# All parts of a matmul stream's operands at one offset from their weights, and a norm product of 64 rows

## The chip, the core and the metric

The kernel runs on one core of a Trainium2 chip. The metric is the time of one execution on the device in microseconds (us); the median over several executions is given, and one execution is profiled. The core's engines are TensorE (PE, with its weight loads as PEld), VectorE (DVE), ScalarE (ACT), GpSimd (POOL) and SyncE (SP), which work beside each other and wait for one another through semaphores. Operands lie in SBUF, 128 partitions wide; TensorE writes to PSUM, whose eight tiles of 128x512 are called bank here.

## The reference

256 tokens of 1024 features run through two blocks, all in float32. The first is one layer: a gated delta rule (4 heads) and a linear recurrence (512 wide) side by side, an output projection, then a feed-forward part. The second puts 16 meta tokens in front (272 tokens) and has two layers of gated feed-forward, mixer, gated feed-forward. Cut to what matters here:

```python
def rmsnorm(x, w):
    return x * rsqrt(mean(x * x, axis=-1) + 1e-6) * w

# first block
x = x + concat(gdn(h), lru(h)) @ w_out          # h = rmsnorm(x) @ w_in, split
x = x + relu(rmsnorm(x) @ w_ff1) ** 2 @ w_ff2   # ff1: 1024 -> 4096, ff2: 4096 -> 1024
x = rmsnorm(x)

# second block, for each of two layers; gate, up: 1024 -> 2816, down: 2816 -> 1024
def swiglu(x, w_gate, w_up, w_down):
    return (silu(x @ w_gate) * (x @ w_up)) @ w_down
h = concat(meta, x)
h = h + 0.5 * swiglu(rmsnorm(h), ...)
h = h + mixer(rmsnorm(h))     # q, k, v, a, b, gs, gc = u @ w_in; attention; convolution; w_out
h = h + 0.5 * swiglu(rmsnorm(h), ...)
return rmsnorm(h)[16:]
```

## The kernel before

Features lie on the partitions and tokens along the columns, so a dense layer is a row of jobs, each for 128 output features: `job` (line 508) takes a bank, and for each block k of 128 input features it issues three matmuls (L534 to L536). The weights are the stationary operand (128x128) and the tokens the moving one, 256 or 272 columns wide. The three are needed because each float32 value is split in two parts of a shorter format, a high part and a low one: high weight times high token (L534), high times low (L535), low times high (L536). These 11136 matmuls are called the stream. In the second layer's mixer and after it only 256 tokens are left, except for a, b, k and v.

Weights come from HBM in chunks of 1 MB at most (`raw`, three buffers, queue of SP). ACT rounds a unit of up to 8 blocks into `wh`, and DVE, or POOL for some units, subtracts it from the raw weights into `wl`. The slots of `wh` and `wl` are 4096 bytes a partition each, one block takes 512 bytes, and the program's allocation puts every slot, and so every block, at 192 modulo 256 bytes.

The moving operands lie in two kinds of places, made by the class `XS`, which has one tensor for the high part and one for the low.

- `places` (lines 671 to 674): the pairs x00/x01 and x10/x11 for the normed tokens. They are handed out in turn. A block takes 320 columns (1280 bytes) with 272 tokens, 256 columns (1024 bytes) with 256.
- `hid`: the hidden features of a feed-forward part, in a pool that is opened at the phase's start, the high part first and the low part behind it.

`SKEW` and `HSKEW` put some columns (of 4 bytes) ahead of the data in each tensor. From the allocation of the program before, the start of each part less the start of its weights, modulo 256 bytes:

| stage (start in the profile, us) | tokens | operand | high part | low part |
|---|---|---|---|---|
| first block's input projection, 7 | 256 | x00/x01 | 192 | 192 |
| its output projection, 141 | 256 | x10/x11 | 192 | 64 |
| ff1, 175 | 256 | x00/x01 | 192 | 192 |
| ff2, 268 | 256 | hid | 192 | 64 |
| layer 1: first gate and up, 359 | 272 | x10/x11 | 192 | 64 |
| first down, 494 | 272 | hid | 192 | 0 |
| mixer: projections, 559 | 272 | x00/x01 | 192 | 192 |
| mixer: out of attention and convolution, 696 | 272 | x10/x11 | 192 | 64 |
| mixer: last projection (o2), 725 | 272 | x00/x01 | 192 | 192 |
| second gate and up, 752 | 272 | x10/x11 | 192 | 64 |
| second down, 886 | 272 | hid | 192 | 64 |
| layer 2: first gate and up, 951 | 272 | x00/x01 | 192 | 192 |
| first down, 1083 | 272 | hid | 192 | 128 |
| mixer: a, b, k, v, 1149 | 272 | x10/x11 | 192 | 64 |
| mixer: q, gc, gs, 1176 | 256 | x10/x11, 16 columns on | 0 | 128 |
| mixer: out of attention and convolution, 1283 | 256 | x00/x01 | 192 | 192 |
| mixer: last projection (o2), 1306 | 256 | x10/x11 | 192 | 64 |
| last gate and up, 1338 | 256 | x00/x01 | 192 | 192 |
| last down, 1459 | 256 | hid | 192 | 0 |

The stages follow one another without a break in the stream, except where a norm or a mixer's small matmuls come in between.

A norm has two steps on TensorE, both in float32. `tok_sums` (line 590) sums the squares over the features with a column of ones. A few DVE operations on a column of 128 tokens make the factor of each token. `to_rows` (line 599) then spreads these factors over all partitions: for each block of tokens a product of the factors, broadcast to 128 columns, with the unit matrix `ident`. A float32 product runs as two passes of weight load and matmul. With 256 tokens there are two blocks of 128, so four passes; with 272, three blocks (16, 128, 128). The stream goes on meanwhile with the next stage's matmuls, since the factor is only applied when a bank is emptied; the calls of the norm stand inside it. `to_rows` with 256 tokens is called at line 725 (first norm), by `norm_rows` for ff1 (line 1328), for the layer norm of the second mixer (line 1572) and for the last gate (line 1747), and at line 1761 for the last norm, where nothing follows but the output.

The order of the work is written out by the emitter itself: `op` books each instruction's estimated time on a clock of its engine, `mm` does so for the small matmuls, and after each block of the stream `tick` lets those flows (generators that evacuate banks, split operands, and so on) go on that these clocks call ready.

Of the kernel before, what the change touches and what calls it, by code (L numbers as in the profile page):

```python
# [7 lines left out]
F32 = mybir.dt.float32  # L8
F32R = mybir.dt.float32r
# [7 lines left out]
T1 = 256  # L17
T2 = T1 + NM
KD = 8
FF1 = 32  # L20
FF2 = 22
# [1 line left out]
MIX1 = 17100  # L23
MIX2 = 16200
XW = 320
SKEW = ((64, 0), (0, 32))
HSKEW = {"ff1": (56, 32), (0, 0): (56, 16), (1, 0): (56, 32), (0, 1): (56, 48), (1, 1): (56, 16)}
LEAD = 3
MINLEAD = 2
RAW = 3  # L30
# [195 lines left out]
def tile_hybrid_blocks(  # L226
# [13 lines left out]
    const = ctx.enter_context(tc.tile_pool(name="const", bufs=1))  # L240
# [12 lines left out]
    def op(eng, cost):  # L253
        f = cur[0]
        start = max(clk[eng], f.t + (LAT if f.eng != eng else DEP if eng == "V" else 0.0))
        clk[eng] = f.t = start + cost
        f.eng = eng

    def size(ap):
        n = 1  # L260
        for d in ap.shape[1:]:
            n *= d
        return n
# [54 lines left out]
    def mm(out, lhsT, rhs, start=True, stop=True):  # L318
        nc.tensor.matmul(out, lhsT, rhs, start=start, stop=stop)  # L319
        op("P", (4 * max(size(lhsT), size(rhs)) if rhs.dtype == F32 else size(lhsT)) / 2400)  # L320
# [98 lines left out]
    phase = ExitStack()  # L419
# [16 lines left out]
    ident = M[:, 0]  # L436
    tri = M[:, 1]

    def cv(name, i=None):
        o, w = CST[name]  # L440
        return C[:, o:o + w] if i is None else C[:, o + i:o + i + 1]
# [157 lines left out]
    def to_rows(r, n, out=None):  # L599

        b = free_banks.pop(0)
        for i, o in enumerate(starts(n)):
            e = min(128, (*starts(n), n)[i + 1] - o)
            mm(b[:, o:o + e], r[0:e, i:i + 1].to_broadcast([e, 128]), ident[0:e, 0:e])
        if out is None:
            return b
        cp(out, b[:, 0:n])
        give(b)
# [60 lines left out]

    places = []  # L670
    for i in range(2):
        both = [const.tile([128, SKEW[i][j] + KD * XW], F32R, name=f"x{i}{j}") for j in range(2)]
        places.append(tuple(b[:, a:] for a, b in zip(SKEW[i], both)))
    const.tile([128, 32], F32, name="gap")

    def X(k):
        return H[:, k, NM:T2]
# [61 lines left out]
    f = start_flow(first_norm())  # L739
# [521 lines left out]
    for i, (c, t) in enumerate(ORDER1):  # L1261
        off = {"q": 0, "k": 4, "v": 8}.get(c, 0)
        b = job(c.upper(), xa, T1)
# [46 lines left out]
    for m in range(0, KD, 2):  # L1310
        if len(free_banks) < 3:
            force(lambda: len(free_banks) >= 3)
        b = free_banks.pop(0)
# [4 lines left out]
    for m in range(0, KD, 2):  # L1318
        b = held[m // 2]
# [7 lines left out]
    phase.close()  # L1327
    start_flow(norm_rows(acc1[:, 0:T1], T1, 1.0 / 1024, 1e-6, R[:, 0:T1], [ev_sq2], ev_r2))
    phase = ExitStack()
    hid = XS(T1, FF1, phase.enter_context(tc.tile_pool(name="ff1", bufs=1)), "hid", pad=HSKEW["ff1"])  # L1330

    def do_ff1(b, m):
        us = yield from slot()
# [79 lines left out]
    ff1_phase = phase  # L1413


    def swiglu(x, ev_r, o, n, next_g, old_phase, skew, final=False):

        old_phase.close()
        phase = ExitStack()
        hid = XS(n, FF2, phase.enter_context(tc.tile_pool(name="ff2", bufs=1)), "hid", pad=HSKEW[skew])  # L1420
        first = T2 - x.n

        def half(ev):
# [30 lines left out]
        ev_sq = Event()  # L1454
        force(lambda: ev5.t is not None and (final or ev_h.t is not None))
        for m in range(KD):
            b = job("down", hid, n)
# [287 lines left out]
    def norm_of(n, ev_sq):  # L1745
        ev = Event()
        start_flow(norm_rows(acc1[:, 0:n], n, 1.0 / 1024, 1e-6, R[:, 0:n], [ev_sq], ev, RC[:, 0:len(starts(n))]))
        return ev

    x, ph, ev_r = xc, ff1_phase, ev_r3  # L1750
    for layer in range(2):
        o = NM * layer
        n = T2 - o
        x, ev_sq, ph = swiglu(x, ev_r, 0, T2, lambda m: cv(f"mix_norm_2.{layer}", m), ph, (0, layer))
        x, ev_sq, ph = mixer(x, norm_of(T2, ev_sq), layer, lambda m: cv(f"ffn2_norm_2.{layer}", m), ph)
        x, ev_sq, ph = swiglu(x, norm_of(n, ev_sq), o, n, lambda m: cv("ffn1_norm_2.1", m), ph, (1, layer), final=layer == 1)
        if layer == 0:
            ev_r = norm_of(n, ev_sq)
    force(lambda: not flows)
# [109 lines left out]
```

## Time and profile before

| | |
|---|---|
| median of 3 runs | 1536.48 us (1528.25 to 1539.7) |
| the profiled execution | 1534.88 us |
| its span, first to last instruction | 1533.2 us |
| mean granted clock of TensorE | 0.989 |
| HBM read | 245.63 MB |
| share of the 16 DMA engines in the weights' queue | 45.3% |
| ACT rounding weights, 128x1024, x370 | 388.0 us |
| DVE splitting weights, 128x1024, x345 | 427.7 us |

A page of the profile gives the busy time of each engine over the span, then the span in 40 slices, then the chain of work that ended last, and the costliest groups of instructions. A line of a window names its start and end, its length, and for each engine the busy time in it and in brackets the number of instructions that touch it; behind these stand the granted clock of TensorE (1.00 is full), the share of the DMA engines, and GB/s. A line of the timeline has the start, the length, the engine, the line of the kernel, the operation, what it writes and reads, and its shapes. Matmuls are pipelined, so their recorded lengths overlap; the distance from one start to the next is what counts.

### The profile page before, as it was taken

Reading aid. Unit: us, or ns where it says so; the run is one execution under the profiler, and the core shown is the slowest. Engines: PE = TensorE matmul, PEld = TensorE weight load, DVE = VectorE, ACT = ScalarE, POOL = GpSimd, SP = SyncE. Lnnn points to the kernel's source line nnn. Section 1 sums busy time; section 2 is a strip of 40 time slices with the busy share of each in tenths; the row PEclk is TensorE's granted clock in tenths of the full one; section 3 lists DMA queues with packets and bytes.
Section 4 is the critical chain, followed back from the end, with each engine's and each line's share of the span. In section 5 each row is a group of like instructions: output and inputs, shape, how many; then the busy total and the mean of one; then the engine's idle time right before and its main releaser. Section 6 shows DMA issues by size and latency. Waiting matters only on the chain. (4 is left out here: it accounts for less than half of the span.)

```text
span 1533.2 us, 29451 instructions
## 1 busy us (share of the span) xinstructions
PE 1490.7 (97%) x12120; PEld 1470.4 (96%) x12120; DVE 1075.5 (70%) x1882; ACT 802.5 (52%) x1365; POOL 196.4 (13%) x236
## 2 busy tenths in 40 slices
PE   7999999999999999999999999999999999899997
PEld 7888999999999999998999999999999989899997
DVE  5986876667666568998866555666558997776654
ACT  4568666544544445555644444444444655555542
POOL 3330300000000012234400000000003235400000
PEclk8999999999999999999999999999999999999998
DMA  5412455554545544433545454554554423455551
GB/s 220 144 56 84 154 204 189 174 190 141 215 166 174 178 171 144 156 114 111 177 182 188 162 177 160 192 184 171 176 186 149 155 110 138 152 207 193 187 181 71
DMA packets 36376, 248.58 MB, mean 162 GB/s; under 512 B 3984, under 2 KB 5264, under 8 KB 12304
## 3 DMA queue, kind: packets, MB, share of 16 engines
q1 hardware_dynamic: 35248, 245.50, 45.3%
q8 instruction: 95, 1.56, 0.4%
q10 hardware_dynamic: 992, 1.19, 0.2%
q14 instruction: 41, 0.34, 0.1%
HBM read 245.63 MB, written 1.05 MB: 161 GB/s over the span
## 5 line engine op out<-in xcount | busy, mean ns | idle before, releaser
L534 PE MATMUL bank<-x,wh 128*128 128x272 f32 (+1 forms) x2752 | 795.8, 289 | 10.7 <-ACT x L276 9.8
L535 PE MATMUL bank<-x,wh 128*128 128x272 f32 (+1 forms) x2752 | 785.3, 285 | 6.5 <-DVE x L288 5.9
L536 PE MATMUL bank<-x,wl 128*128 128x272 f32 (+1 forms) x2752 | 786.8, 286 | 4.2 <-DVE wl L288 3.3
L288 DVE TENSOR_TENSOR wl<-raw,wh 128x1024 fp32r<-128x1024 f32 (+4 forms) x453 | 531.0, 1173 | 191.0 <-PE bank L536 159.5
L276 ACT ACTIVATE wh<-raw 128x1024 fp32r<-128x1024 f32 (+4 forms) x510 | 494.4, 975 | 268.0 <-issue 135.0
L534 PEld LDWEIGHTS bank<-x,wh 128*128 128x128 f32 x2752 | 523.5, 190 | 14.0 <-ACT x L276 10.8
L535 PEld LDWEIGHTS bank<-x,wh 128*128 128x128 f32 x2752 | 524.2, 190 | 9.7 <-DVE x L288 8.0
L536 PEld LDWEIGHTS bank<-x,wl 128*128 128x128 f32 x2752 | 522.0, 190 | 5.5 <-DVE wl L288 4.4
L536 PE MATMUL bank<-hid,wl 128*128 128x272 f32 (+1 forms) x960 | 273.1, 285 | 0.0
L535 PE MATMUL bank<-hid,wh 128*128 128x272 f32 (+1 forms) x960 | 273.0, 284 | 0.0
L534 PE MATMUL bank<-hid,wh 128*128 128x272 f32 (+1 forms) x960 | 272.4, 284 | 0.0
L535 PEld LDWEIGHTS bank<-hid,wh 128*128 128x128 f32 x960 | 181.3, 189 | 0.0
L536 PEld LDWEIGHTS bank<-hid,wl 128*128 128x128 f32 x960 | 180.8, 188 | 0.0
L534 PEld LDWEIGHTS bank<-hid,wh 128*128 128x128 f32 x960 | 180.4, 188 | 0.0
L493 POOL TENSOR_TENSOR wl<-raw,wh 128x512 fp32r<-128x512 f32 (+3 forms) x57 | 106.4, 1878 | 191.9 <-PE bank L536 89.7
L288 DVE TENSOR_TENSOR tmp<-bank,R 128x272 f32<-128x272 f32 (+1 forms) x184 | 78.9, 430 | 66.6 <-PE bank L536 65.8
L276 ACT ACTIVATE tmp<-tmp 128x272 f32<-128x272 f32 (+1 forms) x140 | 59.3, 425 | 114.8 <-DVE tmp L288 78.6
L299 DVE SCALAR_TENSOR_TENSOR bank<-arena,C,bank 128x272 f32<-128x272 f32 (+1 forms) x232 | 102.5, 492 | 3.7 <-ACT bank L276 2.5
L1482 POOL MEMSET arena<- 64x1088 f32 (+1 forms) x4 | 3.9, 976 | 769.0 <-PE bank L536 769.0
L288 DVE TENSOR_TENSOR hid<-tmp,hid 128x272 fp32r<-128x272 f32 (+1 forms) x120 | 51.7, 433 | 38.0 <-ACT hid L276 38.0
L276 ACT ACTIVATE x<-H,C 128x272 fp32r<-128x272 f32 (+2 forms) x64 | 30.0, 487 | 84.7 <-DVE H L288 84.3
L276 ACT ACTIVATE hid<-tmp 128x272 fp32r<-128x272 f32 (+1 forms) x120 | 51.0, 426 | 42.3 <-DVE tmp L288 40.6
(200 smaller groups left out, 950.5 us busy)
## 6 DMA issues: line engine op xcount, KB each, us to landing
raw<-in_w_dram SPq DMA_DIRECT2D x187, 1024.0 KB, 4.8
raw<-in_w_dram SPq DMA_DIRECT2D x32, 960.0 KB, 4.7
raw<-in_w_dram SPq DMA_DIRECT2D x16, 896.0 KB, 4.6
raw<-in_w_dram SPq DMA_DIRECT2D x2, 512.0 KB, 5.9
H<-in_xt_dram SPq DMA_DIRECT2D x1, 544.0 KB, 6.6
LG<-in_lgw_dram SPq DMA_DIRECT2D x1, 512.0 KB, 6.1
out_dram<-H SPq DMA_DIRECT2D x2, 256.0 KB, 2.3
LM<-in_cm_dram SPq DMA_DIRECT2D x1, 320.0 KB, 5.1
```

Of the source, the lines that this page charges most:

```text
L276: nc.scalar.activation(out, in_, func, scale=scale, **kw)
L288: nc.vector.tensor_tensor(out=out, in0=a, in1=b, op=fn)
L299: nc.vector.scalar_tensor_tensor(out=out, in0=a, scalar=s, in1=b, op0=op0, op1=op1)
L493: nc.gpsimd.tensor_tensor(out=lo[:, 0:n], in0=raw[c][:, o:o + n], in1=wh[i][:, 0:n].bitcast(F32), op=SUB)
L534: nc.tensor.matmul(acc, h[:, s], xh, start=first and done == 0, stop=False)
L535: nc.tensor.matmul(acc, h[:, s], xl, start=False, stop=False)
L536: nc.tensor.matmul(acc, lo[:, s], xh, start=False, stop=last and done == total - 1)
L1482: nc.gpsimd.memset(QZ[i].f[64 * (1 - i):64 * (1 - i) + 64], 0.0)
```

## The change

It has two parts. The first puts the high and the low part of every moving operand at one offset from the weights, 192 bytes modulo 256. `SKEW` and `HSKEW` go. The pairs x00/x01 and x10/x11 get tensors without columns ahead, behind a gap of 64 columns (256 bytes); x11, so far 128 bytes further on, now starts like the other three. In `hid` the low part has no pad any more, where it had 32, 16, 32, 48 and 16 columns in the five feed-forward parts; the high part keeps its 56. All that lies behind the pairs moves down by 256 bytes. q, gc and gs of the second mixer still begin 16 columns into a block, so that both their parts are at 0.

The second part is in `to_rows`: with 256 tokens the last block's product is made as two, one for tokens 64 to 127 of the block, which reads all 128 rows, and then one for its tokens 0 to 63, which reads 64 rows. What they compute is the same, since the unit matrix has only zeros in what is left out.

```diff
-SKEW = ((64, 0), (0, 32))
-HSKEW = {"ff1": (56, 32), (0, 0): (56, 16), (1, 0): (56, 32), (0, 1): (56, 48), (1, 1): (56, 16)}
...
         for i, o in enumerate(starts(n)):
             e = min(128, (*starts(n), n)[i + 1] - o)
-            mm(b[:, o:o + e], r[0:e, i:i + 1].to_broadcast([e, 128]), ident[0:e, 0:e])
+            parts = [(0, e, 0, e)]
+            if n == T1 and o + e == n:
+                parts = [(0, e, e // 2, e), (0, e // 2, 0, e // 2)]
+            for p0, p1, s0, s1 in parts:
+                mm(b[:, o + s0:o + s1], r[p0:p1, i:i + 1].to_broadcast([p1 - p0, 128]), ident[p0:p1, s0:s1])
...
     for i in range(2):
-        both = [const.tile([128, SKEW[i][j] + KD * XW], F32R, name=f"x{i}{j}") for j in range(2)]
-        places.append(tuple(b[:, a:] for a, b in zip(SKEW[i], both)))
-    const.tile([128, 32], F32, name="gap")
+        if i == 0:
+            const.tile([128, 64], F32, name="gap")
+        places.append(tuple(const.tile([128, KD * XW], F32R, name=f"x{i}{j}") for j in range(2)))
...
-    hid = XS(T1, FF1, phase.enter_context(tc.tile_pool(name="ff1", bufs=1)), "hid", pad=HSKEW["ff1"])
+    hid = XS(T1, FF1, phase.enter_context(tc.tile_pool(name="ff1", bufs=1)), "hid", pad=(56, 0))
...
-        hid = XS(n, FF2, phase.enter_context(tc.tile_pool(name="ff2", bufs=1)), "hid", pad=HSKEW[skew])
+        hid = XS(n, FF2, phase.enter_context(tc.tile_pool(name="ff2", bufs=1)), "hid", pad=(56, 0))
```

More of the change, by code (lines that the diff above doesn't have):

```diff
@@ L1413, in tile_hybrid_blocks, with swiglu @@
     ff1_phase = phase
-    def swiglu(x, ev_r, o, n, next_g, old_phase, skew, final=False):
+    def swiglu(x, ev_r, o, n, next_g, old_phase, final=False):
         old_phase.close()
         phase = ExitStack()
-        hid = XS(n, FF2, phase.enter_context(tc.tile_pool(name="ff2", bufs=1)), "hid", pad=HSKEW[skew])
+        hid = XS(n, FF2, phase.enter_context(tc.tile_pool(name="ff2", bufs=1)), "hid", pad=(56, 0))
         first = T2 - x.n
@@ L1753, in tile_hybrid_blocks @@
         n = T2 - o
-        x, ev_sq, ph = swiglu(x, ev_r, 0, T2, lambda m: cv(f"mix_norm_2.{layer}", m), ph, (0, layer))
+        x, ev_sq, ph = swiglu(x, ev_r, 0, T2, lambda m: cv(f"mix_norm_2.{layer}", m), ph)
         x, ev_sq, ph = mixer(x, norm_of(T2, ev_sq), layer, lambda m: cv(f"ffn2_norm_2.{layer}", m), ph)
-        x, ev_sq, ph = swiglu(x, norm_of(n, ev_sq), o, n, lambda m: cv("ffn1_norm_2.1", m), ph, (1, layer), final=layer == 1)
+        x, ev_sq, ph = swiglu(x, norm_of(n, ev_sq), o, n, lambda m: cv("ffn1_norm_2.1", m), ph, final=layer == 1)
         if layer == 0:
```

## The prediction

> **What bounds the kernel now.** I read the page first: the busy times, the clock line and the chain that ended last. Its columns are those of the page.
>
> ```profile
> span 1533.2 us, 29451 instructions
> PE 1490.7 (97%) x12120; PEld 1470.4 (96%) x12120; DVE 1075.5 (70%) x1882; ACT 802.5 (52%) x1365; POOL 196.4 (13%) x236
> PEclk8999999999999999999999999999999999999998
> PE bank L534 4%; PE bank L535 4%; PE bank L536 4%; PE bank L319 0%; DVE H L288 0%; POOL acc L311 0%; ACT wh L276 0%; DVE tmp L288 0%; ACT acc L276 0%; DVE rn_t L288 0%; DVEq L1863 0%; ACT tmp L276 0%; ACT rn_y L276 0%; DVE RC L299 0%; DVE rn_s L295 0%
> ```
>
> TensorE is busy nearly all the time at an almost full granted clock, and the three stream products of L534 to L536 lead the chain. So the end is set by how closely these follow each other. The list of groups with shapes kept apart gives their numbers; each line has two sisters of the same count (the other two products), so a count is to be taken three times.
>
> ```profile
> L534 PE MATMUL bank<-x,wh 128*128 128x272 f32 x1600 | 463.1, 289 | 1.3 <-ACT x L276 1.3
> L534 PE MATMUL bank<-x,wh 128*128 128x256 f32 x1152 | 332.7, 289 | 9.4 <-ACT x L276 8.5 <-ACT arena L276 0.9
> L534 PE MATMUL bank<-hid,wh 128*128 128x272 f32 x528 | 151.0, 286 | 0.0
> L534 PE MATMUL bank<-hid,wh 128*128 128x256 f32 x432 | 121.5, 281 | 0.0
> ```
>
> The busy time of one (some 285 ns) isn't its cost, since they overlap. I therefore asked for windows of 60 us inside stages without a break: the number in brackets behind PE counts the products in each, and one hangs over the edges, so the pace is 60.28 us divided by it.
>
> ```profile
> core 0: us, PE busy (x) PEld busy (x) DVE busy (x) ACT busy (x) POOL busy (x), PEclk, DMA share, GB/s
> 190.00:250.00 60.00, 60.00 (x512) 60.00 (x511) 42.06 (x67) 39.81 (x68) 0.00 (x0) 1.00 0.56 197
> 280.00:340.00 60.00, 60.00 (x512) 60.00 (x511) 38.60 (x59) 29.95 (x43) 0.00 (x0) 1.00 0.52 178
> 400.00:460.00 60.00, 60.00 (x485) 60.00 (x483) 35.93 (x50) 29.14 (x41) 0.00 (x0) 1.00 0.49 176
> 495.00:555.00 60.00, 60.00 (x485) 60.00 (x484) 36.25 (x53) 27.57 (x38) 0.00 (x0) 1.00 0.52 182
> 800.00:860.00 60.00, 60.00 (x484) 60.00 (x484) 36.19 (x51) 29.03 (x41) 0.00 (x0) 1.00 0.51 178
> 888.00:948.00 60.00, 60.00 (x484) 60.00 (x483) 35.99 (x51) 26.46 (x38) 0.00 (x0) 1.00 0.52 181
> 965.00:1025.00 60.00, 60.00 (x489) 60.00 (x488) 36.50 (x52) 29.56 (x42) 0.00 (x0) 1.00 0.55 192
> 1085.00:1145.00 60.00, 60.00 (x484) 60.00 (x483) 36.22 (x52) 27.79 (x38) 0.00 (x0) 1.00 0.53 181
> 1380.00:1440.00 60.00, 60.00 (x532) 60.00 (x531) 39.00 (x56) 31.47 (x45) 0.00 (x0) 1.00 0.54 194
> 1460.00:1520.00 60.00, 60.00 (x506) 60.00 (x505) 31.65 (x44) 26.27 (x37) 0.00 (x0) 1.00 0.38 129
> ```
>
> Offsets below are those of the table of stages above (low part from its weights). At 272 columns the five stages whose low part is off 192 (400, 495, 800, 888, 1085) hold 484.4 on average, 124.4 ns each, whether it lies at 64, 0 or 128; the one with both parts at 192 (965) holds 489, 123.3 ns. At 256 columns the two stages with all at 192 differ: the last gate stage (1380) holds 532, 113.3 ns, ff1 (190) holds 512, 117.7 ns. Mixed ones hold 512 (ff2) and 506 (last down, 119.1 ns). So equal offsets at 256 columns have two paces, and something ahead of the stage picks one.
>
> What picks it shows where ff1 is broken for the norm: the matmuls' timeline before and after the product that spreads the norm (L319), and a window behind it.
>
> ```profile
> 183.44 0.28 PE L535 MATMUL bank<-x,wh 128*128 128x256 f32 x1
> ...
> 186.28 0.28 PE L536 MATMUL bank<-x,wl 128*128 128x256 f32 x1
> 186.39 0.60 PE L319 MATMUL bank<-M,nr 128*128 128x128 f32 x4
> 186.75 0.36 PE L534 MATMUL bank<-x,wh 128*128 128x256 f32 x1
> 186.96 0.28 PE L535 MATMUL bank<-x,wh 128*128 128x256 f32 x1
> 188.00:193.00 5.00, 5.00 (x45) 5.00 (x44) 4.75 (x9) 4.91 (x11) 0.00 (x0) 1.00 0.58 210
> ```
>
> Between 183.44 and 186.28 lie 25 steps: 113.6 ns. Behind the product 5.28 us / 45 = 117 ns, and it stays so to the stage's end. The same operands, the same weights' slots; only the restart differs. Elsewhere the stream restarts behind a product of 64 rows:
>
> ```profile
> 130.81 0.68 PE L319 MATMUL bank<-arena 64*64 64x64 f32 x8 [0.31 <-ACT arena L276]
> 131.42 0.39 PE L534 MATMUL bank<-x,wh 128*128 128x256 f32 x1
> 131.64 0.28 PE L535 MATMUL bank<-x,wh 128*128 128x256 f32 x1
> 130.81 0.54 PEld L319 LDWEIGHTS bank<-arena 64*64 64x64 f32 x8 [0.51 <-ACT arena L276]
> 131.42 0.19 PEld L534 LDWEIGHTS bank<-x,wh 128*128 128x128 f32 x1
> 132.00:137.00 5.00, 5.00 (x47) 5.00 (x46) 4.53 (x12) 4.29 (x7) 0.00 (x0) 1.00 0.56 210
> ```
>
> Here the stream's load waits 0.07 us beyond the product's loads (130.81 + 0.54 = 131.35), the restart is later, and the pace is the fast one (5.28 / 47 = 112 ns). It is one clear case, of the same shape in rows.
>
> **The change part by part.** The profiled execution took 1534.88 us, 1.7 us more than its span and 1.60 below the median of 1536.48; I reckon from it.
>
> *272 columns.* x10/x11 feed 2688 of the 3 x 1600 products (both gate stages of layer 1, 2 x 1056; the outputs of its attention and convolution, 192; a, b, k, v of the second mixer, 384), hid 3 x 528 = 1584. All 4272 go from 124.4 to 123.3 ns: 1.17 ns by the unrounded counts, **-5.0 us**. Bounds: the edge count is good to half a product, 0.13 ns, so 4.5 to 5.5.
>
> *ff1.* The new last product has 64 rows, so I take the fast restart: the 693 products behind it (of 768; 48 and 27 come before) gain 117.7 - 113.3 = 4.4 ns, **-3.1 us**. Ends: 0 if the slow pace stays, and 3.1.
>
> *ff2.* Offset 64 becomes 192 and the stage follows ff1 without a break, so it takes over ff1's pace: 768 x 4.4 = **-3.4 us**, or 0 if it locks slow (its present pace is the slow one, 512).
>
> *Last down.* 0 becomes 192 behind a fast gate stage: 528 x (119.1 - 113.3) = **-3.1 us**; if slow, 528 x 1.4 = 0.7.
>
> *Last gate.* Fast already; the new product ahead of it can only keep it (0) or lose 996 x 4.4 = 4.4. I take 0, by the row at 132.
>
> *The other 256-column stages on x10/x11.*
>
> ```profile
> 161.00:171.00 10.00, 10.00 (x87) 10.00 (x86) 6.75 (x12) 6.38 (x14) 6.14 (x5) 1.00 0.59 211
> 1271.50:1276.50 5.00, 5.00 (x45) 5.00 (x44) 3.74 (x10) 2.43 (x7) 0.94 (x2) 1.00 0.59 213
> 1306.00:1336.00 30.00, 24.22 (x179) 23.42 (x178) 22.46 (x33) 15.19 (x30) 13.75 (x10) 0.89 0.45 162
> ```
>
> The first block's output projection (161) runs at 10.28 / 87 = 118.2 ns; fast it would save 192 x 4.9 = 0.9. o2 of the second mixer (1306) would save as much, but TensorE is idle 5.8 of 30 us there, so most would turn into waiting. Between 0 and 1.8 for both, I take **-0.8 us**. In the second mixer q, gc and gs (480 products) read 16 columns, 64 bytes, further on: both parts end at 0 from their weights, and nothing in this profile runs so. They now take 5.28 / 45 = 117 ns. The ends are 113.3 and 119.1 ns, -1.9 to +0.9 us; the nearest row, with one part at 0, is 119.1 at a fixed high part, so I take no change.
>
> *The product.* It becomes one of 128 rows over half the columns and one of 64 rows: two more passes of load and product. A call costs now what these loads show (four passes from 186.28 to 186.73, 0.11 each), the last call at a halved clock 0.93 for four:
>
> ```profile
> 186.28 0.52 PEld L319 LDWEIGHTS bank<-M,nr 128*128 128x128 f32 x4
> 186.73 0.19 PEld L534 LDWEIGHTS bank<-x,wh 128*128 128x128 f32 x1
> 1525.67 0.93 PEld L319 LDWEIGHTS bank<-M,RC 128*128 128x128 f32 x4 [1.29 <-DVE RC L299]
> ```
>
> Two passes are 0.22; the later restart adds some 0.1 (the stream's load at 131.42 comes 0.20 behind the start of the last of eight, against 0.11 here). Four calls in the stream at 0.33 and the last, on the tail with nothing beside it, at 0.5: **+1.8 us**. Ends: 0 where the call falls into a wait, and 2.5.
>
> *Moves.* The pad and the gap change addresses of what lies behind by a multiple of 256 bytes; no instruction, DMA or wait is added elsewhere, and no queue is passed. The emitter books 0.21 us per `mm`, so its clock for TensorE runs 0.21 us ahead after each call and a flow may be emitted a step earlier or later. All waits of TensorE's own list are small, its largest being
>
> ```profile
> PE bank L534 <- ACT x L276: 9.8, 3, 7.2
> ```
>
> so I put -2 to +2 us on that and take 0. What would be late next is the splitting of weights: DVE needs 39.00 of 60 us at the fast pace (1380) without a wait, and ff1's 42.06 of 60 becomes 43.7 at that pace. That covers it.
>
> Sum: 5.0 + 3.1 + 3.4 + 3.1 + 0.8 - 1.8 = 13.6; 1534.88 - 13.6 = **1521.3 us**, 0.99% below the median of 1536.48.
>
> A rule weighed against this. The timeline shows a load starting with the product before it, so both read at once:
>
> ```profile
> 187.07 0.28 PE L536 MATMUL bank<-x,wl 128*128 128x256 f32 x1
> 187.08 0.19 PEld L534 LDWEIGHTS bank<-x,wh 128*128 128x128 f32 x1
> ```
>
> The Trainium skill, "TensorE: Matmul & The Clock Gate", section "Part 2: What happens when you issue a matmul", says that the loads and the streamed operand have a read port each, so that loading the next weights takes nothing from the running product. By that rule addresses wouldn't matter and the time would be that of the second rival below. The trace disagrees: the shape is the same at 484 and at 489, and at 506 and 532.
>
> **The rivals.**
> 1. *A lock is missed.* The paces at 256 columns hang on steps of a few ns (0.21 us from first to second product at 186.75, 0.22 at 131.42). ff1 stays slow and ff2 with it: 1521.3 + 6.5 = 1527.8; or ff2 or the last down falls out at its start: 1524.7 and 1523.7. For it: one operand set showed both paces. Against: the row at 132, and the last gate's 60 us unbroken at one pace.
> 2. *Offsets don't set the pace.* Then nothing is gained and the five products cost: 1534.88 + 1.8 = 1536.7, slower than the profile. For it: ff1 is slow with all at 192. Against: six 272-column stages sort by offset. It decides if 400 to 460 us still holds 485.
> 3. *The 64-row product locks slow.* Gains are the 272 columns' 5.0 and 0.7 in the last down; the last gate loses 4.4, the products 1.8: 1535.4, slower than the profile by 0.5. Its point: the last gate's 60 us at 512 in place of 532. Against: the row at 132.
>
> **How the numbers follow.** Forecast 0.62, rival 1 0.24, rival 2 0.06, rival 3 0.08. About 1% is what a measurement of this kernel can tell from no change: 1521.1 from the median. The bounds of the unknown costs (second mixer -1.9 to +0.9, order 2, products -1.8 to +0.7) put the forecast some 5 us either way, and a stretch at half clock, as in the 0.89 at 1306, moves a run by 1 or 2 more. So 1515 below; above, rival 1 whole with 2 us more, 1530; left out are rivals 2 and 3 and the edges. The forecast lies at the border of 1%: 0.40 of its 0.62 on the faster side, since each fast lock that I counted half (o2, output projection, second mixer) adds to it; all else is within 1%, but for 0.03 of slower, a reordering beyond my 2 us.
>
> **What would show it.** The 60 us windows: 489 at 272 columns everywhere, 532 in ff1, ff2, last gate and last down. L319 in the norms with a 64-row form and six passes. Wrong would be 484 or 485 at 272 columns, or 512 in the last gate.

## The result, and the profile after

The changed kernel takes 1520.21 us (median of 9 runs, 1515.92 to 1524.16), the kernel before 1533.79 us in the same rounds (median of 9, 1525.12 to 1539.7). The ratio is 0.992, with a 95% interval of 0.990 to 0.995. The profiled execution of the changed kernel took 1520.58 us, 14.30 less than that of the kernel before; all that follows compares these two. Two slow runs of the experiments below, one of the offsets alone at 5177 us and one of the sums on DVE at 7906 us, are left out of the medians and counts given there.

In the code of the changed kernel the three stream products are L532 to L534, the norm's products L317, ACT's line is L274 and DVE's L286. First the page: its span, busy times, clock line and the chain that ended last.

```profile
span 1518.9 us, 29471 instructions
PE 1478.2 (97%) x12130; PEld 1457.5 (96%) x12130; DVE 1075.8 (71%) x1882; ACT 802.7 (53%) x1365; POOL 198.3 (13%) x236
PEclk9999999999999999999999999999999999999999
PE bank L532 26%; PE bank L534 26%; PE bank L533 26%; PE bank L317 4%; DVE bank L297 2%; DVE wl L286 2%; DVE arena L286 2%; DVE arena L297 2%; ACT arena L274 1%; DVE arena L313 1%; PE bank L321 1%; DVE x L286 1%; ACT wh L274 1%; DVE tmp L286 0%; POOL acc L309 0%
```

TensorE has ten more passes (12130 for 12120: two more in each of five calls) and is busy 12.5 us less. DVE, ACT and POOL do what they did. So most of the time came out of the stream itself. The windows of the changed kernel, columns as in the prediction, show where:

```profile
161.00:171.00 10.00, 10.00 (x91) 10.00 (x90) 7.03 (x12) 6.68 (x15) 6.18 (x5) 1.00 0.60 211
195.00:255.00 60.00, 60.00 (x532) 60.00 (x531) 41.96 (x67) 39.37 (x66) 0.00 (x0) 1.00 0.55 193
280.00:340.00 60.00, 60.00 (x532) 60.00 (x532) 40.32 (x62) 30.89 (x45) 0.00 (x0) 1.00 0.54 193
400.00:460.00 60.00, 60.00 (x488) 60.00 (x488) 36.39 (x51) 29.42 (x41) 0.00 (x0) 1.00 0.50 176
888.00:948.00 60.00, 60.00 (x489) 60.00 (x488) 35.70 (x53) 26.63 (x39) 0.00 (x0) 1.00 0.48 165
1085.00:1140.00 55.00, 55.00 (x448) 55.00 (x447) 34.04 (x48) 25.90 (x35) 0.00 (x0) 1.00 0.52 181
1380.00:1440.00 60.00, 60.00 (x532) 60.00 (x531) 39.07 (x56) 31.39 (x45) 0.00 (x0) 1.00 0.53 192
1450.00:1505.00 55.00, 55.00 (x488) 55.00 (x487) 30.91 (x42) 26.14 (x37) 0.00 (x0) 1.00 0.40 140
```

These stages have the pace that was forecast: 488 or 489 products in 60 us at 272 columns (400, 888; at 1085 it is 55.28 us / 448 = 123.4 ns), and at 256 columns 532 in ff1, ff2 and the last gate, and 55.28 / 488 = 113.3 ns in the last down. The output projection (161) is at 10.28 / 91 = 113.0 ns.

But the stages' lengths don't all follow. Two rows of the kernel before stand ahead of the two of the changed kernel here: ff1 from its first product on, then the second mixer's last projection (o2).

```profile
175.00:269.00 94.00, 91.94 (x782) 91.74 (x781) 67.40 (x118) 60.12 (x103) 4.70 (x5) 1.00 0.54 192
1305.90:1337.60 31.70, 25.92 (x194) 25.12 (x193) 23.05 (x34) 15.91 (x31) 14.49 (x11) 0.89 0.42 154
...
174.00:268.00 94.00, 91.42 (x777) 91.09 (x776) 67.39 (x116) 60.49 (x103) 4.84 (x6) 0.96 0.54 191
1298.00:1325.90 27.90, 25.71 (x200) 24.99 (x199) 24.39 (x35) 16.94 (x32) 15.84 (x11) 0.94 0.51 186
```

In the same 94 us TensorE gets through five instructions fewer (777 for 782), two of which the norm has more, so ff1 is behind by seven stream products in spite of the faster pace: the clock is 0.96 where it was 1.00. And o2, for which nearly nothing was forecast, is done sooner: 27.9 us hold 200 products, where 31.7 held 194. With the six more (0.7 us) that is 4.5 us. The clock's share says how long it ran at half: 31.7 x 0.11 x 2 = 7.0 us before, 27.9 x 0.06 x 2 = 3.3 after.

The loss in ff1 lies around the norm. The first two rows are the kernel before (the sums' product on TensorE's timeline, with the idle time ahead of it in brackets, and a window behind it), the others the changed kernel.

```profile
182.78 0.61 PE L319 MATMUL bank<-ones,acc 128*128 128x1 f32 x4 [2.06 <-POOL acc L311]
182.70:186.30 3.60, 3.52 (x31) 3.52 (x32) 2.53 (x13) 0.00 (x0) 0.13 (x2) 1.00 0.82 291
...
181.97 1.01 PE L317 MATMUL bank<-ones,acc 128*128 128x1 f32 x4 [2.58 <-POOL acc L309]
182.90:188.50 5.60, 5.60 (x27) 5.60 (x28) 5.13 (x18) 1.71 (x5) 0.00 (x0) 0.50 0.41 167
188.65 0.91 PE L317 MATMUL bank<-M,nr 128*128 128x128 f32 x6
189.50 0.38 PE L532 MATMUL bank<-x,wh 128*128 128x256 f32 x1
189.72 0.28 PE L533 MATMUL bank<-x,wh 128*128 128x256 f32 x1
```

TensorE is done with what stands ahead of the norm's sums at 179.39 us (181.97 - 2.58), 1.33 earlier than before (182.78 - 2.06 = 180.72), but POOL's additions for them come only 0.81 earlier: the wait grew from 2.06 to 2.58 us. Behind it the granted clock is half (0.50): the sums' product takes 1.01 us instead of 0.61, and the 27 products up to the norm's product take 5.6 us instead of 27 x 0.1136 = 3.1. Then the product itself: from its first pass to the stream's restart it is 189.50 - 188.65 = 0.85 us, where the prediction's rows have 186.75 - 186.39 = 0.36. So it costs 0.49 more, not 0.33.

The gain in o2 hangs on a race between two engines. Kernel before, then changed kernel; the engine stands behind the start and the length, and the last row of each is a window with the granted clock:

```profile
1314.58 2.38 POOL L493 TENSOR_TENSOR wl<-raw,wh 128x1024 fp32r<-128x1024 f32 x1 [2.76 <-ACT wh L276]
1314.68 2.57 DVE L288 TENSOR_TENSOR x<-arena,x 128x256 fp32r<-128x256 f32 x1
1317.30 0.58 PE L535 MATMUL bank<-x,wh 128*128 128x256 f32 x1 [3.62 <-DVE x L288]
1311.50:1314.90 3.40, 2.18 (x19) 1.97 (x17) 1.93 (x4) 2.76 (x4) 0.64 (x2) 1.00 0.58 205
...
1307.82 0.42 DVE L286 TENSOR_TENSOR x<-arena,x 128x256 fp32r<-128x256 f32 x1
1307.85 5.99 POOL L491 TENSOR_TENSOR wl<-raw,wh 128x1024 fp32r<-128x1024 f32 x2 [2.88 <-PE bank L534]
1308.88 2.68 DVE L286 TENSOR_TENSOR wl<-raw,wh 128x1024 fp32r<-128x1024 f32 x1 [0.65 <-ACT wh L274]
1304.70:1308.10 3.40, 3.40 (x19) 3.40 (x17) 1.96 (x3) 2.82 (x4) 0.52 (x2) 0.50 0.59 186
```

Before, POOL's split of weights starts 0.10 us ahead of DVE's operand for o2. DVE's operation, else 0.42 us, then lasts 2.57 and ends 0.29 us after POOL's; TensorE waits 3.62 us for it, and the stretch at half clock is the longer one. After, DVE is 0.03 us ahead of POOL; now a split of weights is held up (2.68 us), for which TensorE doesn't wait. The Trainium skill, "SBUF — State Buffer", section "Who interferes with whom", says the same in general: DVE with two SBUF inputs and GpSimd share a port that one of them locks for its whole instruction, and the order of issue decides who is held up. The trace agrees: 2.38 us of POOL, and 2.57 in place of 0.42 on DVE.

By these rows, where the half clock falls tips the race. DVE's operand starts 8.8 us after o2's first product in both kernels. In the changed kernel the clock is half from 5.7 to 9.1 us after that first product; TensorE is then late with products that POOL's split waits for (2.88 us for PE in its row), and POOL starts behind DVE. In the kernel before the clock is full at that place, POOL waits for ACT alone (2.76 us) and starts first.

### The profile page after: what moved, and what is told of

It reads as the page before. It is cut to its first block, busy times and chain, and to the rows that moved or that the text cites. A ratio compares the mean times of both kernels' runs of the same rounds, so it can differ in the third digit from the quotient of the medians.

```text
span 1518.9 us, 29471 instructions
## 1 busy us (share of the span) xinstructions
PE 1478.2 (97%) x12130; PEld 1457.5 (96%) x12130; DVE 1075.8 (71%) x1882; ACT 802.7 (53%) x1365; POOL 198.3 (13%) x236
## 4 chain that ended last, share of the span: by engine, by line
PE 83%; DVE 12%; ACT 3%; issue 1%; POOL 1%; DMA 0%; DVEq 0%; SPq 0%; ACTq 0%; POOLq 0%
PE bank L532 26%; PE bank L534 26%; PE bank L533 26%; PE bank L317 4%; DVE bank L297 2%; DVE wl L286 2%; DVE arena L286 2%; DVE arena L297 2%; ACT arena L274 1%; DVE arena L313 1%; PE bank L321 1%; DVE x L286 1%; ACT wh L274 1%; DVE tmp L286 0%; POOL acc L309 0%
## 5 line engine op out<-in xcount | busy, mean ns | idle before, releaser
L532 PE MATMUL bank<-x,wh 128*128 128x272 f32 (+1 forms) x2752 | 796.1, 289 | 10.8 <-ACT x L274 9.8
L534 PE MATMUL bank<-x,wl 128*128 128x272 f32 (+1 forms) x2752 | 784.1, 285 | 5.6 <-DVE wl L286 4.7
L286 DVE TENSOR_TENSOR wl<-raw,wh 128x1024 fp32r<-128x1024 f32 (+4 forms) x453 | 532.6, 1177 | 183.4 <-PE bank L534 152.6
L274 ACT ACTIVATE wh<-raw 128x1024 fp32r<-128x1024 f32 (+4 forms) x510 | 494.5, 976 | 257.0 <-issue 136.1
L532 PEld LDWEIGHTS bank<-x,wh 128*128 128x128 f32 x2752 | 523.8, 190 | 14.4 <-ACT x L274 10.9
L534 PEld LDWEIGHTS bank<-x,wl 128*128 128x128 f32 x2752 | 523.5, 190 | 6.7 <-DVE wl L286 5.6
L534 PE MATMUL bank<-hid,wl 128*128 128x272 f32 (+1 forms) x960 | 270.6, 282 | 0.0
L532 PE MATMUL bank<-hid,wh 128*128 128x272 f32 (+1 forms) x960 | 270.6, 282 | 0.0
L532 PEld LDWEIGHTS bank<-hid,wh 128*128 128x128 f32 x960 | 180.6, 188 | 0.0
L534 PEld LDWEIGHTS bank<-hid,wl 128*128 128x128 f32 x960 | 180.6, 188 | 0.0
L286 DVE TENSOR_TENSOR tmp<-bank,R 128x272 f32<-128x272 f32 (+1 forms) x184 | 78.7, 429 | 64.8 <-PE bank L534 63.9
L274 ACT ACTIVATE tmp<-tmp 128x272 f32<-128x272 f32 (+1 forms) x140 | 59.3, 425 | 114.6 <-DVE tmp L286 78.4
L286 DVE TENSOR_TENSOR hid<-tmp,hid 128x272 fp32r<-128x272 f32 (+1 forms) x120 | 51.7, 433 | 38.3 <-ACT hid L274 38.3
L274 ACT ACTIVATE hid<-tmp 128x272 fp32r<-128x272 f32 (+1 forms) x120 | 51.0, 426 | 42.3 <-DVE tmp L286 40.7
L274 ACT ACTIVATE x<-H,C 128x272 fp32r<-128x272 f32 (+2 forms) x64 | 30.0, 486 | 81.6 <-DVE H L286 81.2
```

The lines of the kernel that those rows point to most:

```text
L274: nc.scalar.activation(out, in_, func, scale=scale, **kw)
L286: nc.vector.tensor_tensor(out=out, in0=a, in1=b, op=fn)
L532: nc.tensor.matmul(acc, h[:, s], xh, start=first and done == 0, stop=False)
L534: nc.tensor.matmul(acc, lo[:, s], xh, start=False, stop=last and done == total - 1)
```

## The experiments

All edits are against the changed kernel. Paces are worked out from windows as in the prediction. Two restarts pick a pace: the one behind the norm's product in ff1, which ff2 inherits, and the one in the last gate, which the last down inherits.

**Each part by itself.** The first kernel has the new offsets and the old `to_rows`:

```diff
-            parts = [(0, e, 0, e)]
-            if n == T1 and o + e == n:
-                parts = [(0, e, e // 2, e), (0, e // 2, 0, e // 2)]
-            for p0, p1, s0, s1 in parts:
-                mm(b[:, o + s0:o + s1], r[p0:p1, i:i + 1].to_broadcast([p1 - p0, 128]), ident[p0:p1, s0:s1])
+            mm(b[:, o:o + e], r[0:e, i:i + 1].to_broadcast([e, 128]), ident[0:e, 0:e])
```

> The offsets of the changed kernel with the norm's product as it was (128 rows, four passes). My theory: offsets set the pace at 272 columns and in mixed 256-column stages, the 64-row product only picks the pace after a restart. Then all 272-column windows of 60 us hold 489 (123.3 ns), ff2 and the last down are at 532 or 512 (113.3 or 117.7 ns) as the stage ahead of them happens to be, never at 506; ff1 and the last gate are each at 512 or 532 by chance. Time: the five products' cost comes back (2.4 us by the changed kernel's trace), and some of ff1 + ff2 (6.5 us) and last gate + last down (6.7 us) is lost: 1518 to 1531 us, about 1525. Rival (the product does it all): 484 at 272 columns and a time as before, 1534 us.

The second has the new `to_rows` and the old `SKEW`, `HSKEW` and places.

> The offsets of the kernel before with the new product of 64 rows. My theory: ff1 and the last gate, whose operands lie at 192 in both kernels, are both at 532 in 60 us; ff2 stays at 512, the last down at 506, the 272-column stages on x10/x11 and hid at 484 or 485. Time: 3.1 us gained in ff1 against a run that has it slow, 2.4 us paid for the products: 1531 to 1537 us, no difference to before that three rounds can show. Rival (offsets don't matter, the product picks every stage's pace): 489 and 532 everywhere and 1520 us.

With the offsets alone the median is 1531.12 us (9 runs), just above the 1518 to 1531 expected, ratio 0.997 (0.995 to 1.000). The profiled execution was by chance one at the fast pace in ff1 and the last gate, 1521.19 us; the other runs lie at 1525 to 1537. Its windows at 272 columns hold 488 or 489 products, the first row below. With the product alone it is 1531.70 us (5 runs, 1527.68 to 1533.77), ratio 0.997 (0.995 to 0.998). Its windows stand behind:

```profile
400.00:460.00 60.00, 60.00 (x489) 60.00 (x488) 36.22 (x52) 29.25 (x41) 0.00 (x0) 1.00 0.50 177
...
195.00:255.00 60.00, 60.00 (x532) 60.00 (x531) 42.10 (x68) 40.02 (x67) 0.00 (x0) 1.00 0.57 204
280.00:340.00 60.00, 60.00 (x512) 60.00 (x511) 38.06 (x58) 29.69 (x42) 0.00 (x0) 1.00 0.55 191
400.00:460.00 60.00, 60.00 (x485) 60.00 (x484) 36.19 (x51) 29.00 (x41) 0.00 (x0) 1.00 0.49 176
```

With the product alone ff1, whose operands were at 192 before, is fast; ff2 and the 272 columns, whose low parts aren't, stay where they were. So at 272 columns it is the offsets that set the pace, and not the product. Each part alone gives 0.3%, both together 0.8%: the offsets make a fast pace possible in ff2 and the last down, the product makes it likely that the stage ahead of them hands it on.

**What of the product does it.** Three forms of the last block: two halves that both read 128 rows; the two halves in the other order, so that the product of 128 rows is last; and 32 rows in place of 64.

```diff
-                parts = [(0, e, e // 2, e), (0, e // 2, 0, e // 2)]
+                parts = [(0, e, e // 2, e), (0, e, 0, e // 2)]       # two halves
+                parts = [(0, e // 2, 0, e // 2), (0, e, e // 2, e)]  # swapped
+                parts = [(0, e, 32, e), (0, 32, 0, 32)]              # 32 rows
```

> The changed kernel, but the second half-product reads all 128 rows too: the same number of passes and columns, no 64-row load. What it computes is the same. If the rows pick the pace (the stream's load has to wait for the end of a product of another row count), the first stream matmul after the product starts some 0.03 us after the last pass as it did before, not 0.20, and ff1 and the last gate fall to 512 or 532 by chance; time 1519 to 1531 us. If the two further passes or their 64 columns do it, both are at 532 as in the changed kernel, and the time is that of the changed kernel less some 1 us.

> The changed kernel with the two half-products in the other order: first the one of 64 rows, then the one of 128 rows, so that the stream restarts behind 128 rows. The same two loads and products are made. If the restart behind a product of other row count is what makes the fast pace likely, the runs spread again as with the offsets alone: steps of 6.5 us (ff1 with ff2) and 6.7 us (last gate with last down), 1516 to 1532 us with a median near 1526. If it is enough that such a product is anywhere in the norm, the runs lie as those of the changed kernel, 1515.9 to 1524.2 us with a median near 1520.

> The last block's product is made as one for its tokens 32 to 127, which reads all 128 rows, and then one for tokens 0 to 31, which reads 32 rows; all else is as in the changed kernel. Theory (the row count of the last product ahead of the stream picks the pace, and the fewer rows it has, the surer the fast one): the profile shows ff1, ff2, the last gate and the last down at 532 or 533 products in 60 us, and the timed runs lie within 1515 to 1524 as those of the changed kernel did, none near 1528 or above. Rival (a fast restart is an even chance whatever the product, as with 128 rows last): the runs spread in steps of 6.5 us from 1515 to 1537 with a median near 1528, and one of the two restarts in the profile holds 509 to 512.

Two halves of 128 rows: 1522.46 us, ratio 0.990 (0.985 to 0.994), but out of 1514.79, 1517.5, 1527.42 and 1528.09; in the profile ff1 is fast and the last gate slow (512 in 60 us). Swapped: 1528.12 us (12 runs, 1516.7 to 1536.48), ratio 0.999 (0.996 to 1.001), and both stages slow in the profile:

```profile
195.00:255.00 60.00, 60.00 (x512) 60.00 (x511) 40.47 (x65) 38.23 (x65) 0.00 (x0) 1.00 0.52 187
1380.00:1440.00 60.00, 60.00 (x512) 60.00 (x511) 37.75 (x54) 30.06 (x42) 0.00 (x0) 1.00 0.53 189
```

The swapped kernel has the same products and passes as the changed one. Only the last of them differs, and with it the restart. TensorE's loads there, the swapped kernel first:

```profile
187.05 1.08 PEld L317 LDWEIGHTS bank<-M,nr 128*128 128x128 f32 x6
188.06 0.19 PEld L532 LDWEIGHTS bank<-x,wh 128*128 128x128 f32 x1
...
188.54 0.89 PEld L317 LDWEIGHTS bank<-M,nr 128*128 128x128 f32 x6
189.49 0.19 PEld L532 LDWEIGHTS bank<-x,wh 128*128 128x128 f32 x1
```

Behind 128 rows the stream's load starts before the product's loads end (188.06 against 187.05 + 1.08 = 188.13); behind 64 rows it starts 0.06 us after they end. With 32 rows the median is 1521.11 us (1519.39 to 1521.3, 6 runs), ratio 0.991 (0.989 to 0.993), and both ff1 and the last gate hold 532. The changed kernel was run again beside it:

> The changed kernel unaltered, beside the two runs before on one chip, as their measure and as more throws of its two restarts. Theory (64 rows make the fast restart likely, not certain): ten fast restarts of twelve so far, so some two thirds of the runs within 1515 to 1524 and the others 3 to 7 us above; median 1518 to 1523. Rival (the nine runs so far were fast by their chip's state, and the row count does nothing): median near 1528, as with 128 rows last.

It took 1521.72 us in the median (6 runs), ratio 0.992 (0.989 to 0.995), but with two runs off the others, 1524.8 and 1529.4: four of six within 1515 to 1524, as expected of a likely, not a certain, fast restart. Over all kernels, whose operands in ff1 and the last gate all lie at 192, the restarts in the profiles and the timed runs sort by the last product:

| last product | kernels | fast restarts in profiles | runs of at most 1524.5 us |
|---|---|---|---|
| 128 rows | before (restarts only), offsets only, two halves, swapped | 4 of 8 | 4 of 25 |
| 64 rows | changed (twice), and below sums on DVE and second mixer shifted; for restarts also product only and both maps of offsets | 12 of 14 | 22 of 26 |
| 32 rows | 32 rows, 32 rows and shift | 4 of 4 | 12 of 12 |

So the theory stands in a weaker form: a last product of fewer than 128 rows doesn't force the fast pace, it raises its chance, and behind 64 rows 2 of 14 restarts were slow. That 32 rows are surer than 64 isn't shown by so few.

Three things mix into the table. The runs are from several series, in which the kernel before had medians from 1529.78 to 1536.3 us. A time of at most 1524.5 us isn't the same as two fast restarts: it holds the race in o2 and the half clocks as well. In ff1 the half clock goes with the pace too: of the eight traces with half clock just ahead of the norm's product seven restart fast, of the five without it two, and both slow restarts behind 64 rows are among these five. No run here separates that from the rows. In the last gate the clock is full well ahead of the restart in all thirteen traces; there 2 of 4 are fast behind 128 rows and 9 of 9 behind fewer.

**Is it equality, or 192?** Two kernels put both parts of each operand at one offset, but at others than 192. The first, with x10/x11 at 128 and hid at 64, 0, 64, 128 and 128 in order:

```diff
+HPAD = [72, 24, 40, 40]
...
-        if i == 0:
-            const.tile([128, 64], F32, name="gap")
+        const.tile([128, (64, 48)[i]], F32, name=f"gap{i}")
...
+    const.tile([128, 16], F32, name="gap2")
...
-    hid = XS(T1, FF1, phase.enter_context(tc.tile_pool(name="ff1", bufs=1)), "hid", pad=(56, 0))
+    hid = XS(T1, FF1, phase.enter_context(tc.tile_pool(name="ff1", bufs=1)), "hid", pad=(24, 0))
...
-        hid = XS(n, FF2, phase.enter_context(tc.tile_pool(name="ff2", bufs=1)), "hid", pad=(56, 0))
+        hid = XS(n, FF2, phase.enter_context(tc.tile_pool(name="ff2", bufs=1)), "hid", pad=(HPAD.pop(0), 0))
```

> Both parts of each operand at one offset, but another than 192: x10/x11 at 128 (so q, gc and gs of the second mixer at 192), hid at 64 in ff2, 0, 64 and 128 in the three downs with 272 columns, 128 in the last down; x00/x01 stay at 192. If equality of the two parts is what counts, the 272-column stages all stay at 489 in 60 us and ff2 and the last down at 532. If 192 itself counts, the moved stages fall: at 272 columns to 484 or lower, at 256 columns to 512 or lower (0 and 0 gave 119.7 ns in the second mixer, 504 in 60 us), while q, gc and gs rise from 119.7 ns to 113.3 or 117.7. I lean to the second for 0, and have no view on 64 and 128.

The second in the same way, with x10/x11 at 224 and hid at 32, 32, 96, 160 and 160.

> Equal parts at offsets that are multiples of 32 but not of 64: x10/x11 at 224, hid at 32 (ff2 and the first down), 96, 160 and 160; x00/x01 stay at 192. With 0, 64 and 128 at 125.3, 126.7 and 126.7 ns at 272 columns, against 123.3 at 192, I expect 123.3 to 127 for each of these; none below 123.3 if 192 is the best of all. A stage at 120 ns or less would say that a better offset exists.

One run each, 1538.56 and 1540.16 us. The windows (400 is x10/x11, the others hid; first kernel, then second):

```profile
400.00:460.00 60.00, 60.00 (x476) 60.00 (x475) 35.13 (x51) 28.65 (x40) 0.00 (x0) 1.00 0.50 176
495.00:555.00 60.00, 60.00 (x481) 60.00 (x480) 35.05 (x50) 26.06 (x36) 0.00 (x0) 1.00 0.50 171
888.00:948.00 60.00, 60.00 (x476) 60.00 (x475) 35.21 (x49) 26.50 (x36) 0.00 (x0) 1.00 0.50 177
...
400.00:460.00 60.00, 60.00 (x475) 60.00 (x475) 35.11 (x50) 28.86 (x40) 0.00 (x0) 1.00 0.50 176
495.00:555.00 60.00, 60.00 (x479) 60.00 (x479) 35.12 (x50) 26.12 (x36) 0.00 (x0) 1.00 0.50 171
888.00:948.00 60.00, 60.00 (x481) 60.00 (x480) 34.99 (x48) 26.35 (x36) 0.00 (x0) 1.00 0.50 176
1085.00:1140.00 55.00, 55.00 (x448) 55.00 (x448) 33.12 (x47) 25.21 (x35) 0.00 (x0) 1.00 0.52 177
1450.00:1505.00 55.00, 55.00 (x475) 55.00 (x474) 32.53 (x46) 28.06 (x39) 0.00 (x0) 1.00 0.53 183
```

| both parts at | 0 | 32 | 64 | 96 | 128 | 160 | 192 | 224 |
|---|---|---|---|---|---|---|---|---|
| products in 60 us, 272 columns | 481 | 479 | 476 | 481 | 476 | 448 in 55 | 489 | 475 |
| ns each | 125.3 | 125.8 | 126.6 | 125.3 | 126.6 | 123.4 | 123.3 | 126.9 |

Equality isn't what counts: both parts at 64 or 128 are slower (126.6 ns) than one at 192 and one elsewhere (124.4). What counts is where each part lies, and at 272 columns 160 is as good as 192. At 256 columns it isn't: the last down with both parts at 160 (the last row) runs at 55.28 / 475 = 116.4 ns behind a last gate at 113.3, where the changed kernel's last down keeps 113.3. No run moves the weights, so whether the place counts from the weights or by itself is open. In the first of the two kernels ff1, whose operands and product were those of the changed kernel, restarted slow (512 in 60 us).

**The half clock ahead of ff1.** The last four additions for the norm's sums go to DVE instead of POOL:

```diff
-        start_flow(residual(b, m, xb, cv("norm_mlp_w", m), acc1[:, 0:T1], ev_sq2, o=NM, add=pt, free=False))
+        start_flow(residual(b, m, xb, cv("norm_mlp_w", m), acc1[:, 0:T1], ev_sq2, o=NM, add=pt if m < 4 else tt, free=False))
```

and the same in the call for `m + 1`.

> The changed kernel; the sums of squares of the last four of eight blocks before ff1's norm are added on VectorE, no longer on GpSimd. In the changed kernel's trace TensorE stood 2.6 us for these sums ahead of ff1 and then ran 27 products at half clock (some 2.7 us). My theory (that pair is where ff1's gain went): the wait falls by 1 to 2 us, the half clock ahead of ff1 goes, and the time by 1 to 4.5 us: 1516 to 1519 us. Rival: VectorE, 91% busy there, delays weights or operands instead: no gain, 1520 to 1522 us.

```profile
182.90:188.50 5.60, 5.60 (x48) 5.46 (x48) 5.26 (x19) 3.31 (x8) 0.00 (x0) 1.00 0.60 199
195.00:255.00 60.00, 60.00 (x512) 60.00 (x511) 40.18 (x65) 37.77 (x64) 0.00 (x0) 1.00 0.56 194
```

The wait and the half clock are gone (1.00 over the whole stretch), as meant. But ff1 restarted slow in this execution, 512, and the time was 1522.26 us; the median is 1522.26 (5 runs), ratio 0.992 (0.989 to 0.995). In that trace ff1 takes 91.88 us from its first product to ff2's, 2.47 less than in the changed kernel, in spite of the slow pace. So the loss of some 3 us was rightly placed, while a gain in the time isn't shown. Of the thirteen traces, the half clock followed the wait for these sums in eight and not in four others with waits of 2.05 to 2.14 us; in three of the eight the wait was 2.06 us as well. So the wait's length alone doesn't decide. The Trainium skill, "TensorE: Matmul & The Clock Gate", section "Part 1: The HAM clock gate", says that the gate looks at free-running windows of about 3.4 us, of which an idle one halves the clock. With that agree the lengths, 3.3 us in o2 after and 7.0 before, some one and two windows, and that the same gap costs in one run and not in another; but no wait ahead of ff1 was as long as a window, 2.58 us at most, so an idle window alone doesn't explain these half clocks.

**q, gc and gs at 192.** In the layer whose second mixer has 256 columns, the blocks of its operand start 48 columns later in their 320, so that the 256 tokens lie at 192 and the 272 ones (a, b, k, v) at 128:

```diff
-        nx = None if final else XS(T2)
+        nx = None if final else XS(T2, sh=sh)
...
-        x, ev_sq, ph = swiglu(x, ev_r, 0, T2, lambda m: cv(f"mix_norm_2.{layer}", m), ph)
+        x, ev_sq, ph = swiglu(x, ev_r, 0, T2, lambda m: cv(f"mix_norm_2.{layer}", m), ph, sh=48 * layer)
```

> The changed kernel, but the operands of the second mixer's projections are put 48 columns into their blocks of 320: q, gc and gs (480 products of 256 columns) then lie at 192 where they lay at 0, a, b, k and v (384 products of 272 columns) at 128 where they lay at 192. From the runs so far: 480 x (119.7 - 113.6) = 2.9 us gained, 384 x (126.7 - 123.3) = 1.3 us lost, 1.6 us in all if TensorE sets that stage's end: 1518.6 us, a difference that five rounds may just not show. The trace should show 113 to 114 ns for q, gc and gs, 126.7 for the others. Rival (the mixer waits for VectorE, so TensorE's pace is given back in waits): 1520 us at the same paces.

The same row of 51 products, by its second and its last on the timeline (kernel before, changed kernel, shifted kernel):

```profile
1271.29 0.28 PE L535 MATMUL bank<-x,wh 128*128 128x256 f32 x1
1277.07 0.28 PE L536 MATMUL bank<-x,wl 128*128 128x256 f32 x1
...
1263.77 0.28 PE L533 MATMUL bank<-x,wh 128*128 128x256 f32 x1
1269.64 0.28 PE L534 MATMUL bank<-x,wl 128*128 128x256 f32 x1
...
1259.75 0.28 PE L533 MATMUL bank<-x,wh 128*128 128x256 f32 x1
1265.31 0.28 PE L534 MATMUL bank<-x,wl 128*128 128x256 f32 x1
```

49 steps: 118.0 ns, 119.8 and 113.5. The pace came as meant in this row, but not in all: other rows of the shifted kernel run at 117.8 ns, the slow pace of 192, among them the next one of 26 products. a, b, k and v run at 126.7 ns at 128. From the first of a, b, k and v to o2's first product the shifted kernel takes 157.37 us, the changed one 157.40, so nothing is gained there. The time is 1519.84 us (6 runs, 1515.47 to 1526.49), ratio 0.993 (0.990 to 0.995): no difference to the changed kernel that these runs can tell. The shift and the 32 rows together were tried as the best version:

> The 32-row product of the run before and the shift of the second mixer's operand by 48 columns together, as the version that may beat the changed kernel. Theory: q, gc and gs at 113.3 to 114.1 ns, a, b, k and v at 126.7; the sum of the two, -3 us for 480 products and +1.3 for 384, gives 1517 to 1520 in the median, at most 2 us below the changed kernel. Rival (the second mixer waits for other engines anyway): 1520 to 1522, no difference to the changed kernel on the same chip.

1519.98 us (1518.6 to 1521.67, 6 runs), ratio 0.990 (0.988 to 0.992), beside 1521.11 with the 32 rows alone and 1521.72 for the changed kernel on the same chip. It is the lowest median of the three, but a gain of 1 to 2 us over the changed kernel isn't shown.

## Why the prediction was right, point by point

The time forecast was 1521.3 us from a profile of 1534.88, so 13.6 less; the profile after is 14.3 less. The mechanism was the forecast one, and the paces came as forecast, but for q, gc and gs. That the sum came out so well is in part luck: errors of both signs balanced. A stage's length here is the time from its first product to that of the next stage, before and after.

| term | forecast, us | measured, us | from |
|---|---|---|---|
| 272 columns | -5.0 | -4.5 | 488.5 for 484.4 in 60 us, x4272 |
| ff1's pace | -3.1 | -3.1 | 532 for 512, x693 |
| ff1, wait and half clock | none | +3.4 | 2.58 for 2.06; 1.01 for 0.61; 5.6 for 3.1 us |
| ff2 | -3.4 | -3.4 | length 87.04 for 90.45 |
| last down | -3.1 | -3.1 | length 59.73 for 62.85 |
| output projection and o2's pace | -0.8 | -0.5 | length 33.39 for 33.92 in the first; o2 below |
| q, gc, gs | 0 | +0.9 | 119.8 for 118.0 ns, x480 |
| the product, five calls | +1.8 | +1.5 | 0.49 in each of three; the first and the last call are in the two rows at the end |
| o2 | 0 (order, 2 either way) | -4.5 | length 27.27 for 31.80 |
| ahead of the output projection | none | -0.6 | it starts at 140.41 for 140.99 |
| tail behind the last stream product | none | -0.4 | 11.03 for 11.43 |
| sum | -13.6 | -14.3 | 14.3 between the profiles |

The last two rows stand for stretches that the change didn't mean to touch but for one call of the product each; what made them shorter wasn't taken apart.

- *The offsets* were right: 400 to 460 us holds 488, where the second rival needed 485. The term was a little too large, -4.5 for -5.0: it went by one stage at 489, and the moved ones hold 488.5 on average. The rule of the Trainium skill weighed there gives the loads and the streamed operand a read port each. What the prediction drew from it, that addresses wouldn't matter, is refuted: at one shape the pace runs from 123.3 to 126.9 ns with nothing but the place of the operand. Whether the ports share anything isn't shown, nor by what mechanism a place slows the stream; only the map of offsets is.
- *The output projection* has two paces as well, as the half count allowed: in the profile of the changed kernel when it was run again 110 of its steps take 117.8 ns each, not some 113.
- *The 64-row product* was right in sign. The third rival is out: the last gate holds 532. That the order of the halves, not the split, moves the time is shown by the swapped halves, with one run of 12 at or below 1524.5 us where the sums on DVE and the shifted mixer, run beside it with 64 rows last, have nine of 11. That it does so through the odds of the two restarts is what the profiles say, with the reservation for ff1 above.
- *The product's price* was mis-sized: 0.49 us a call in ff1, the second mixer and the last gate, not 0.33. Four passes lie 0.36 us ahead of the restart before, six lie 0.85 ahead of it after; the step took 0.22 for two passes and 0.1 for the later restart, and 0.17 more came.
- *ff1* was mis-sized where the prediction said that the splitting of weights is late next. Late next were POOL's sums for the norm, ahead of the 693 products that it counted. The faster stream ahead of them ran into a wait of 2.58 us and a half clock behind it; these cost 3.4 us, more than the 3.1 that the pace gained, and with the product's 0.49 the stage is 0.8 us longer (94.35 for 93.55).
- *q, gc, gs* reached the bad end that had been given, +0.9; the step took the nearest row, one part at 0, for both.
- *Moves* ("-2 to +2, I take 0") missed o2: the wait of 3.62 us stood in the trace of the kernel before, and with the half clock behind it it was worth 4.5 us. Of the thirteen traces the kernel before, the offsets alone, the swapped halves and the second map of offsets lost the race there, and the other nine won it. In all nine a half clock starts 4 to 6 us after o2's first product and POOL waits for TensorE; in all four it starts only 9.8 us after it or later, and POOL waits for ACT. No run moves the half clock alone, and what decides where it falls isn't shown. Three of the four that lost have 128 rows last, of the nine that won one has, so whether the change moves these odds is open as well. As the prediction had no such term, that it fell well here is luck: without it the sum would be 9.8 us.
- *Rival 1*, a missed lock, did not show in the profiled execution, but it exists: two slow restarts of ff1 behind 64 rows, one of them (sums on DVE) with ff2 at 192 and slow behind it. A later run of the changed kernel at 1529.4 us would fit its price; that run has no trace.

## What to carry over

Where one engine issues thousands of equal products, work out the pace of each stage from starts in a trace, and hold it against where operand and weights lie in memory: here the place alone moved the pace by 3% at 272 columns (123.3 to 126.9 ns), and the restart by 4% at 256 (113.3 to 117.7). Add up stage lengths as well as paces: a sum that comes out right can hide a stage that lost what another won by chance. A kernel whose runs differ in steps of a fixed size has a stage with two paces; look for what stands just ahead of that stage, and judge an edit by the spread of its runs and not by one profile. When a stage gets faster, ask which producer it now overtakes: the gain of ff1 was eaten by a wait that grew from 2.06 to 2.58 us and by the half clock behind it.

## What the runs showed of the hardware that was not expected

- The pace of 128x128 loads with products of 272 columns depends on the place of the streamed operand, given here from its weights, modulo 256 bytes: 123.3 and 123.4 ns at 192 and 160, 125.3 at 0 and 96, 125.8 at 32, 126.6 to 126.9 at 64, 128 and 224. At 256 columns 160 gave 116.4 ns in the one stage that had it.
- At 256 columns and 192 there are two steady paces, 113.3 and 117.7 ns, and one is kept for hundreds of products. At 272 columns and 192 there are two as well: in layer 1's first gate stage, between the norm's sums and its product, a row of 51 products runs at the slow one in eight of the nine kernels that have that operand at 192, in the ninth (swapped halves) at the fast one. The row's second and last product in the changed kernel, 49 steps of 126.7 ns:

```profile
362.94 0.29 PE L533 MATMUL bank<-x,wh 128*128 128x272 f32 x1
369.15 0.29 PE L534 MATMUL bank<-x,wl 128*128 128x272 f32 x1
```

- Half clock for at least 5.6 us followed a wait of 2.58 us, and in other kernels one of 2.06, though the kernel before had none at that place with 2.06.
- Where the half clock falls goes with which of two other engines is first: in o2 POOL waited for TensorE and let DVE by in all nine traces with half clock ahead of the race, and in none of the four others.
- One DVE operation that starts 0.10 us behind a POOL operation lasts 2.57 us in place of 0.42, and one that starts 0.03 us ahead of it isn't held up.
